# Tokens turned by products with diagonal matrices, in place of scaled tokens turned with the identity, in the opening of a hybrid encoder step

## The chip, the cores and the metric

The kernel runs on one core of one Trainium2 chip. The metric is the device time of that core in microseconds, the median of several runs. Engine names as the profile has them: PE (TensorE's matmuls), PEld (its weight loads), DVE (VectorE), ACT (ScalarE), POOL (GpSimd), SP (the engine that issues most DMAs).

## The reference

One layer of a streaming encoder, for 1024 prompt frames and 32 frames of a running stream, each of 1024 channels. What matters here is its beginning:

```python
def rmsnorm(x, g):
    xf = x.astype(jnp.float32)
    y = xf * lax.rsqrt(jnp.mean(xf * xf, axis=-1, keepdims=True) + EPS) * g.astype(jnp.float32)
    return y.astype(x.dtype)

def mixer_inputs(x, norm_g, w_in, b_f, q_g, k_g):
    h = rmsnorm(x, norm_g)
    cols = lambda a, w: h @ w_in[:, a:a + w]
    ...
    u = cols(OFF_UA, CONV_WIDTH) * jax.nn.sigmoid(cols(OFF_UB, CONV_WIDTH))
```

From h come the queries, keys and values of an attention with forget gates, the input u of a causal convolution of width 31, and gates. Attention and convolution are each gated and projected, mixed, projected once more and added to x. All of it is float32.

## The kernel before

All 1056 frames (tokens) are handled together. The kernel wants h with channels on the partitions, while x comes with tokens on the partitions. So nine tiles `xtok[t]` of 128 tokens x 1024 channels (the ninth has the 32 stream tokens) are loaded, each token is multiplied by the inverse root of its mean square, and each 128 x 128 block is turned on TensorE into PSUM. On the way out of PSUM the norm's gain is put on (`gs`, per channel) and the value is split into two float16 parts: `xh` on ScalarE (L578), and `xl`, the rest, on VectorE (L579). Every projection is then three float16 products per block of 128 channels: wh with xh, wl with xh, wh with xl (`mms`, L183), the weights being split in the same way (`high`, L138; `low`, L141).

The opening overlaps this with the first two projections (the two factors of u for its first 128 channels; weights `ws0`). `x_split(c, ...)` works on chunk c of the tokens: chunk 0 has tiles 0 and 1, chunk 1 tiles 2 to 4, chunk 2 tiles 5 to 8 (`XCH`). For each of the 8 blocks of channels (kt) it turns the chunk's tiles into one PSUM tile (`ptx`; three PSUM buffers in all), takes xh and xl out of it, runs the jobs that are listed for this kt, and then releases the products of earlier kt that have waited long enough in the lists `behind` (`drain`). In this part the order on PE, DVE and ACT is the program's order (`manual_schedule`); GpSimd and SP are ordered by the scheduler. So an instruction of PE, DVE or ACT that waits holds back all that stands behind it on that engine.

The names that the change touches:

- `squares(t)` sums a tile's squares into a column of `rs9`; `root` and `newton` make inverse roots of them in place (L530 to L532, L509 to L511). `rooted(2, 3)` does tiles 2 to 4, `rooted(5, 4)` tiles 5 to 8.
- `scale(t, h)` multiplies half h of the channels of tile t by its roots, in place, on VectorE (L541) or GpSimd (L539). There are 18: tiles 1, 3 and 6 on GpSimd, the others on VectorE.
- the turn: `nc.tensor.transpose` of a block of `xtok` with the identity `ident` (L576).

After the opening come the other projections of u, v, k, q and the gates with the convolution's taps on VectorE beside them, then the attention over heads, the layer norm, and the output projections. Two lines of them are of use for comparison: L1172, which multiplies the attention's probabilities with the values (plain float32), and

```python
    def over_channels(acc, put):
        for c in range(3):
            pm = psT.tile([128, 512], F32, name="psn", tag="T")
            nc.tensor.matmul(pm[:, :CH], ones_f, acc[:, csl(c)], start=True, stop=True)   # L1202
```

where `ones_f`, `mean` and `rstd` are float32 and CH is 352. In L1172 the inner loop runs over c in 0 to 3 and j below 2c + 2, 20 products for each of the 16 heads.

Of the kernel before, what the change touches and what calls it, by code (L numbers as in the profile page):

```python
# [8 lines left out]
F32 = mybir.dt.float32  # L9
# [5 lines left out]
ALU = mybir.AluOpType  # L15
# [38 lines left out]
def build(tc, xT, xt, wv, wf, ckT, cv, clT, stT, vec, cst, yT, kT, vO, lfO, cpT, csT):  # L54
    nc = tc.nc
# [3 lines left out]
    def pool(name, bufs=1, stack=es, **kw):  # L59
        return stack.enter_context(tc.tile_pool(name=name, bufs=bufs, reuse_waits="tile", **kw))  # L60
# [29 lines left out]
    class Batch:  # L90
# [46 lines left out]
        def high(self, i, wh, raw, ks):  # L137
            nc.scalar.mul(wh[:, ks, :], raw[:, ks, :], self.s[:, i:i + 1])  # L138

        def low(self, i, wl, wh, raw, ks):  # L140
            nc.vector.scalar_tensor_tensor(wl[:, ks, :], raw[:, ks, :], self.s[:, i:i + 1], wh[:, ks, :],  # L141
                                           op0=ALU.mult, op1=ALU.subtract)
# [35 lines left out]
    def mms(ps, w, rh, rl, sl, kts=range(KT), first=True, last=True):  # L178
        wh, wl = w[:2]
        n, N = 0, 3 * len(kts)  # L180
        for kt in kts:
            for a, b in ((wh, rh), (wl, rh), (wh, rl)):
                nc.tensor.matmul(ps, a[:, kt, :], b(kt, sl), start=(first and n == 0), stop=(last and n == N - 1))  # L183
                n += 1
# [202 lines left out]
    def pieces(o, n):  # L387

        if o + n <= T:
            return ((slice(0, n), slice(30 + o, 30 + o + n)),)  # L390
        return ((slice(0, T - o), slice(30 + o, 30 + T)), (slice(T - o, n), slice(60 + T, 60 + T + TS)))
# [40 lines left out]
    xip = pool("xip", 1, stack=xi, side="right")  # L432
    vec_t = cp.tile([128, NV], F32, name="vec_t")
    cst_t = xip.tile([128, NCST], F32, name="cst_t")
    xtok = {}
# [53 lines left out]
    ident = cp.tile([128, 128], F32, name="ident")  # L489
# [7 lines left out]
    rs9 = cp.tile([128, 9], F32, name="rs9")  # L497
# [15 lines left out]
    half = slice(0, D // 2), slice(D // 2, D)  # L513
    rows = lambda t: min(128, TT - 128 * t)
# [17 lines left out]
        nc.scalar.activation(y, y, AF.Exp, scale=-0.5)  # L532
        return lambda: newton(rs, v, y)

    def scale(t, h, pool=False):
        r = rows(t)
        x, f = xtok[t][:r, half[h]], rs9[:r, t:t + 1]
        if pool:
            nc.gpsimd.tensor_scalar(x, x, f, 1.0, op0=ALU.mult, op1=ALU.mult)  # L539
        else:  # L540
            nc.vector.tensor_scalar(x, x, f, None, op0=ALU.mult)  # L541

    behind = [], []

    def drain(lags):
        for q, n in zip(behind, lags):
            while len(q) > n:
                q.pop(0)()

    def x_split(c, ws, u, jobs):  # L550


        o, n = XCH[c]
        sl = slice(o, o + n)
        pss = [pj.tile([128, 512], F32, name="pj", tag="pj") for _ in range(2)]

        def project(i, kt):
            mms(pss[i][:, :n], ws[i], X, XL, sl, range(kt, kt + 1), kt == 0, kt == KT - 1)
            if kt < KT - 1:
                return  # L560
            if i == 0:
                for a, b in pieces(o, n):
                    nc.scalar.mul(u[:, b], pss[0][:, a], recs[0].inv)
                return
            nc.vector.tensor_scalar(ua0[:, sl], pss[1][:, :n], recs[1].inv, None, op0=ALU.mult)
            if c == 2:
                for o2, n2, a2 in PCS:
                    b = slice(30 + o2, 30 + o2 + n2)
                    nc.scalar.activation(u[:, b], u[:, b], AF.Sigmoid)
                    nc.vector.tensor_mul(u[:, b], ua0[:, a2:a2 + n2], u[:, b])  # L570

        for kt in range(KT):
            pt = tr.tile([128, 512], F32, name="ptx", tag="tr") if kt % 3 == 2 else st.tile([128, 512], F32, name="ptx", tag="st")
            for j in range((n + 127) // 128):
                r = min(128, n - 128 * j)
                nc.tensor.transpose(pt[:, 128 * j:128 * j + r],  # L576
                                    xtok[o // 128 + j][:r, 128 * kt:128 * kt + 128], ident[:r, :r])
            nc.scalar.mul(xh[:, kt, sl], pt[:, :n], gs[:, kt:kt + 1])  # L578
            nc.vector.scalar_tensor_tensor(xl[:, kt, sl], pt[:, :n], gs[:, kt:kt + 1], xh[:, kt, sl],  # L579
                                           op0=ALU.mult, op1=ALU.subtract)  # L580
            for job in jobs.get(kt, ()):
                job()
            for i in range(2):
                behind[i].append(lambda i=i, kt=kt: project(i, kt))
            drain((2, 5 if c == 0 else 2))
# [16 lines left out]
    def known(i):  # L602
        recs[i].power(psq[:, i + 1:i + 2], 1)
# [11 lines left out]
    top(0)  # L615
    total(1)
    step()
    scale(0, 0)
    scale(1, 0, True)
    scale(1, 1, True)  # L620
    scale(0, 1)
    known(0)
    steps_of = {}

    def rooted(t0, nt):
        steps_of[t0] = root(t0, nt)
# [12 lines left out]
    for f in range(8):  # L639
        if f in (2, 4, 6):  # L640
# [11 lines left out]
    b1 = plan.pop(0)  # L652
    b2 = plan[0]
    x_split(0, ws0, u0, {
        0: [lambda: high(0, 0), lambda: low(0, 0), lambda: top(1), lambda: squares(2, False)],
        1: [lambda: squares(3)],
        2: [lambda: high(0, 1), lambda: low(0, 1)],
        3: [lambda: total(2), lambda: known(1), lambda: squares(4)],
        4: [lambda: high(1, 0), lambda: low(1, 0), lambda: rooted(2, 3), lambda: high(0, 2)],
        5: [lambda: steps_of[2](), lambda: scale(2, 0), lambda: scale(3, 0, True), lambda: scale(4, 0), lambda: low(0, 2)],  # L660
        6: [lambda: scale(3, 1, True), lambda: scale(2, 1), lambda: high(1, 1), lambda: low(1, 1)],
        7: [lambda: scale(4, 1), lambda: high(1, 2), lambda: low(1, 2)]})
    x_split(1, ws0, u0, {
        0: [b1.load, b1.load, lambda: squares(5), lambda: squares(6, False)],
        1: [lambda: squares(7)],
        2: [lambda: squares(8)],
        3: [lambda: rooted(5, 4)],
        4: [lambda: steps_of[5](), lambda: scale(5, 0), lambda: scale(6, 0, True)],
        5: [lambda: scale(7, 0), lambda: scale(8, 0), lambda: scale(6, 1, True)],
        6: [lambda: scale(5, 1), lambda: scale(7, 1)],  # L670
        7: [lambda: scale(8, 1), lambda: b1.stage(0)]})
    x_split(2, ws0, u0, {0: [lambda: b1.stage(1)], 2: [consts], 3: [b1.total, b1.power],
                         4: [lambda: b1.split(0)], 5: [lambda: b1.rest(0, 0), lambda: b1.rest(0, 1)],
                         6: [lambda: b1.rest(0, 2), lambda: b1.split(1)]})
# [994 lines left out]
```

## Time and profile before

| | before |
|---|---|
| time, median of 3 runs | 1346.9 us (1346.65 to 1347.09) |
| profiled execution: its own time | 1345.89 us |
| its span, first to last instruction | 1344.1 us |
| mean granted TensorE clock | 0.996 of full speed |
| PE busy | 1312.6 us (98%) |
| DVE busy | 990.4 us (74%) |
| ACT busy | 719.0 us (53%) |
| POOL busy | 505.8 us (38%) |

The opening is the first 46 us of the span. A row of a time line gives the start in us, the duration in us, the engine, the line of the kernel, the operation, the tiles (out<-in), their shape, how many were merged into the row, and in brackets how long the engine had been idle and what ended the wait. A row of the views by line gives the count and, behind the bar, busy time in us and the mean of one in ns, then idle time in front of it with what ended it. Matmuls overlap, so their durations are longer than the distances between their starts.

### The profile page before, as it was taken

How to read it: one execution, taken by the hardware profiler on the slowest of the kernel's cores; microseconds unless marked ns; L12 is line 12 of the kernel's file. 1: busy time of each engine (PE TensorE's matmuls, PEld its weight loads, DVE VectorE, ACT ScalarE, POOL GpSimd, SP SyncE). 2: the span in 40 equal slices, each digit the busy share in tenths (PEclk: the TensorE clock that was granted, in tenths of full speed). 3: DMA queues.
4: the chain of work that ended last, by engine and by line, in shares of the span. 5: the costliest groups of instructions: out<-in, count | busy, mean ns of one | idle time of the engine just before them, and what ended most of it. 6: DMA issues, size and time to landing. Idle time of an engine off the chain costs nothing.

```text
span 1344.1 us, 24837 instructions
## 1 busy us (share of the span) xinstructions
PE 1312.6 (98%) x9383; PEld 1003.1 (75%) x9383; DVE 990.4 (74%) x1532; ACT 719.0 (53%) x1362; POOL 505.8 (38%) x548
## 2 busy tenths in 40 slices
PE   8999999999999999999889998999999999999999
PEld 5687876666666666667567766777776699999998
DVE  6797879888999997987778866655554489166664
ACT  6644555757676743455555555655555566233320
POOL 2001124547484820243433442222222158255562
PEclk8999999999999999999999999999999999999999
DMA  6343233425352463535644643565452698544462
GB/s 251 98 140 104 93 112 118 139 82 187 95 180 87 162 166 109 160 90 155 165 109 123 186 132 99 147 179 132 131 152 54 240 313 262 176 128 146 142 190 69
DMA packets 113496, 194.97 MB, mean 145 GB/s; under 512 B 34080, under 2 KB 80032, under 8 KB 113376
## 3 DMA queue, kind: packets, MB, share of 16 engines
q1 hardware_dynamic: 113232, 193.31, 46.9%
q8 instruction: 74, 1.21, 0.4%
q14 instruction: 46, 0.38, 0.1%
q10 hardware_dynamic: 144, 0.07, 0.0%
HBM read 127.68 MB, written 65.64 MB: 144 GB/s over the span
## 4 chain that ended last, share of the span: by engine, by line
PE 82%; DVE 9%; ACT 3%; issue 2%; DMA 2%; SPq 1%; POOL 0%; DVEq 0%; ACTq 0%; POOLq 0%
PE pj L183 56%; PE pjv L761 6%; PE pj L1501 6%; PE po L1172 4%; PE ptr L1153 3%; DVE nm L1126 2%; DVE wl L141 2%; DVE y L371 2%; PE psS L1122 2%; PE psS L1121 2%; DMA ga<-s_ga 2%; ACT wh L138 1%; DVE psS L1124 1%; DMA s_q<-qh 1%; PE warm L477 1%
## 5 line engine op out<-in xcount | busy, mean ns | idle before, releaser
L183 PE MATMUL pj<-xh,wh 128*128 128x352 f16 (+2 forms) x1536 | 481.6, 314 | 2.3 <-ACT wh L138 1.4
L183 PE MATMUL pj<-xh,wl 128*128 128x352 f16 (+2 forms) x1536 | 481.2, 313 | 0.7 <-DVE wl L141 0.6
L183 PE MATMUL pj<-xl,wh 128*128 128x352 f16 (+2 forms) x1536 | 480.9, 313 | 0.5 <-DVE xl L579 0.4
L183 PEld LDWEIGHTS <-wh 128*128 128x128 f16 x3072 | 301.5, 98 | 162.1 <-issue 7.1
L371 DVE SCALAR_TENSOR_TENSOR y<-u,vec_t,y 128x1086 f32<-128x1086 f32 x240 | 346.8, 1446 | 12.0 <-ACT y L368 8.9
L1139 POOL TENSOR_SCALAR P<-P,nm 128x128 f32<-128x128 f32 (+7 forms) x128 | 129.9, 1015 | 279.9 <-DVE nm L1138 229.8
L183 PEld LDWEIGHTS <-wl 128*128 128x128 f16 x1536 | 150.5, 98 | 72.0 <-DVE wl L141 1.6
L141 DVE SCALAR_TENSOR_TENSOR wl<-raw,sc,wh 128x384 f16<-128x384 f32 (+1 forms) x192 | 128.2, 693 | 48.3 <-ACT wh L138 48.3
L1133 ACT ACTIVATE P<-psS,nm 128x128 f32<-128x128 f32 (+7 forms) x128 | 95.1, 743 | 113.3 <-DVE nm L1138 70.9
L1126 DVE TENSOR_REDUCE nm<-psS 128x1 f32<-128x128 f32 (+7 forms) x128 | 97.0, 758 | 12.5
L1153 PE MATMUL ptr<-ident,P 128*128 128x128 f32 x576 | 88.6, 276 | 17.3 <-DVE pt L1156 9.2
L175 POOL TENSOR_TENSOR wl<-raw,wh 128x384 fp32r<-128x384 f32 (+1 forms) x51 | 63.3, 1270 | 74.3 <-ACT wh L172 58.6
L1153 PEld LDWEIGHTS ptr<-ident,P 128*128 128x128 f32 x576 | 69.2, 141 | 28.2 <-DVE pt L1156 12.1
L1156 ACT COPY pt<-ptr 128x512 f32<-128x512 f32 (+3 forms) x128 | 64.3, 502 | 44.4 <-PE ptr L1153 43.2
L1121 PE MATMUL psS<-KB,QB 128*128 128x256 f32 (+2 forms) x192 | 81.8, 427 | 0.6 <-ACT P L1133 0.6
L880 POOL TENSOR_TENSOR sql<-sqf,sqh 128x352 fp32r<-128x352 f32 x48 | 57.0, 1187 | 65.8 <-ACT sqh L877 65.8
L138 ACT ACTIVATE wh<-raw,sc 128x1024 f16<-128x1024 f32 (+1 forms) x68 | 73.9, 1091 | 8.2 <-DVE sc L158 7.9
L1172 PE MATMUL po<-pt,V 128*64 128x256 f32 x640 | 72.8, 382 | 2.5 <-ACT pts L1078 1.7
L1124 DVE TENSOR_TENSOR psS<-psS,cmask 128x128 f32<-128x128 f32 x128 | 37.6, 294 | 46.0 <-PE psS L1122 45.6
L906 POOL TENSOR_TENSOR ql<-qn,qh 128x352 fp32r<-128x352 f32 (+1 forms) x48 | 67.8, 1429 | 6.6 <-ACT qh L905 6.5
L761 PE MATMUL pjv<-vwh,xh 128*128 128x260 f16 x256 | 70.1, 274 | 0.0
L761 PE MATMUL pjv<-vwl,xh 128*128 128x260 f16 x256 | 70.0, 273 | 0.0
(271 smaller groups left out, 2532.9 us busy)
## 6 DMA issues: line engine op xcount, KB each, us to landing
raw<-wf SPq DMA_DIRECT2D x92, 512.0 KB
QB<-s_q SPq DMA_DIRECT2D x32, 256.0 KB
KB<-s_k SPq DMA_DIRECT2D x32, 256.0 KB
kT<-qn SPq DMA_DIRECT2D x8, 528.0 KB
s_ga<-t SPq DMA_DIRECT2D x24, 176.0 KB
s_gb<-t SPq DMA_DIRECT2D x24, 176.0 KB
s_ma<-t SPq DMA_DIRECT2D x24, 176.0 KB
s_mb<-t SPq DMA_DIRECT2D x24, 176.0 KB
```

Of the source, the lines that this page charges most:

```text
L138: nc.scalar.mul(wh[:, ks, :], raw[:, ks, :], self.s[:, i:i + 1])
L141: nc.vector.scalar_tensor_tensor(wl[:, ks, :], raw[:, ks, :], self.s[:, i:i + 1], wh[:, ks, :], op0=ALU.mult, op1=ALU.subtract)
L183: nc.tensor.matmul(ps, a[:, kt, :], b(kt, sl), start=(first and n == 0), stop=(last and n == N - 1))
L371: t = nc.vector.scalar_tensor_tensor(y, u[:, i:i + CW], w, y, op0=ALU.mult, op1=ALU.add)
L761: nc.tensor.matmul(ps[:, :VC], a, b, start=(n == 0), stop=(n == 23))
L1121: nc.tensor.matmul(ps[:, b, :wm], QB[:, qsl], KB[:, ksl], start=True, stop=False)
L1126: nc.vector.tensor_reduce(nm[:, 0:1], ps[:, :nb, :w], axis=AX.XY, op=ALU.max, negate=True)
L1133: nc.scalar.activation(P[:, :nk].rearrange("p (b w) -> p b w", b=nb), ps[:, :nb, :w], AF.Exp, bias=nm[:, 0:1], accum_out=nm[:, 1:2])
L1139: nc.gpsimd.tensor_scalar(P[:, :nk], P[:, :nk], nm[:, 2:3], 1.0, op0=ALU.mult, op1=ALU.mult)
L1153: nc.tensor.transpose(pt[:, 128 * j:128 * j + 128], P[:, 128 * (4 * u + j):128 * (4 * u + j) + 128], ident)
L1172: nc.tensor.matmul(po[rows], V[:, j, :], parts[c][:, j, :], start=(c % 2 == 0 and j < 2), stop=(c % 2 == 1 and j >= 2 * c))
L1501: nc.tensor.matmul(pss[c][:, :HC], a[:, k, :], x, start=(not more and kt == 0 and n == 0), stop=(kt == 3 and n == 2), skip_group_check=more)
```

## The change

`scale` and its 18 calls are taken out. In their place `diag(t)` writes a 128 x 128 tile with the roots of tile t on its diagonal (the identity times the root, per partition; 32 x 32 for the last tile), nine in all, on VectorE. A block of `xtok` is then turned and scaled at once, by a plain product with that diagonal tile as the moving operand instead of a turn with the identity. `xtok` itself stays as it was loaded.

```diff
-    def scale(t, h, pool=False):
-        r = rows(t)
-        x, f = xtok[t][:r, half[h]], rs9[:r, t:t + 1]
-        if pool:
-            nc.gpsimd.tensor_scalar(x, x, f, 1.0, op0=ALU.mult, op1=ALU.mult)
-        else:
-            nc.vector.tensor_scalar(x, x, f, None, op0=ALU.mult)
+    diags = {}
+
+    def diag(*ts):
+        for t in ts:
+            r = rows(t)
+            diags[t] = xip.tile([128, 128], F32, name="diag", tag="diag", bufs=9)
+            nc.vector.tensor_scalar(diags[t][:r, :r], ident[:r, :r], rs9[:r, t:t + 1], None, op0=ALU.mult)
...
             for j in range((n + 127) // 128):
                 r = min(128, n - 128 * j)
-                nc.tensor.transpose(pt[:, 128 * j:128 * j + r],
-                                    xtok[o // 128 + j][:r, 128 * kt:128 * kt + 128], ident[:r, :r])
+                t = o // 128 + j
+                nc.tensor.matmul(pt[:, 128 * j:128 * j + r], xtok[t][:r, 128 * kt:128 * kt + 128], diags[t][:r, :r],
+                                 start=True, stop=True)
...
     step()
-    scale(0, 0)
-    scale(1, 0, True)
-    scale(1, 1, True)
-    scale(0, 1)
+    diag(0, 1)
     known(0)
...
-        5: [lambda: steps_of[2](), lambda: scale(2, 0), lambda: scale(3, 0, True), lambda: scale(4, 0), lambda: low(0, 2)],
-        6: [lambda: scale(3, 1, True), lambda: scale(2, 1), lambda: high(1, 1), lambda: low(1, 1)],
-        7: [lambda: scale(4, 1), lambda: high(1, 2), lambda: low(1, 2)]})
+        5: [lambda: steps_of[2](), lambda: diag(2, 3, 4), lambda: low(0, 2)],
+        6: [lambda: high(1, 1), lambda: low(1, 1)],
+        7: [lambda: high(1, 2), lambda: low(1, 2)]})
...
-        4: [lambda: steps_of[5](), lambda: scale(5, 0), lambda: scale(6, 0, True)],
-        5: [lambda: scale(7, 0), lambda: scale(8, 0), lambda: scale(6, 1, True)],
-        6: [lambda: scale(5, 1), lambda: scale(7, 1)],
-        7: [lambda: scale(8, 1), lambda: b1.stage(0)]})
+        4: [lambda: steps_of[5](), lambda: diag(5, 6, 7, 8)],
+        7: [lambda: b1.stage(0)]})
```

## The prediction

> **What bounds the kernel now.** I read the page first, for the bound of the whole, then the chain of waits in order of time for the first 140 us, because the change lies in the first 46 us and the question is whether time lost there comes back later. The page's first part:
>
> ```profile
> PE 1312.6 (98%) x9383; PEld 1003.1 (75%) x9383; DVE 990.4 (74%) x1532; ACT 719.0 (53%) x1362; POOL 505.8 (38%) x548
> ```
>
> TensorE is busy for 98% of the span. What happens in the opening therefore moves the end only by the moment at which TensorE's unbroken work begins. The chain shows that moment (start, duration, what; the lines are those the chain went through):
>
> ```profile
> 19.26 1.33 DVE xtok L541 x2
> 20.59 0.82 DVE wl L141
> ...
> 32.49 0.78 DVE xtok L541 x2
> ...
> 46.08 17.59 PE pj L183 x114
> ```
>
> There are three stages. In chunk 0 the chain runs over VectorE and ScalarE; near its end stand two scales (L541) and a weight low part (L141), and behind them the low part xl of a turned tile (L579), which frees the PSUM buffer for the first turn of chunk 1. In chunk 1 (to 33.86, the first turn of four tiles) the chain again names scales, although TensorE is nearly full, as shown below. In chunk 2 (from 33.86) turns and products alternate on TensorE, and from 46.08 on 114 products follow without a break. So a TensorE microsecond added in chunk 2 arrives at the end whole; a VectorE microsecond removed counts only as far as it made TensorE wait.
>
> **The turn becomes a product: what one costs.** The number of instructions is the first thing to settle. The turns at L576 are 2x8 + 3x8 + 3x8 = 64 of full size (and 8 of 32 rows), and 64 MATMULs stand in the view by shape. Plain float32 products are different: the loop at L1202 has three of them for mean and the view has six MATMULs; the loop at L1172 has 16 heads x 20 = 320 and the view has 640:
>
> ```profile
> L1172 PE MATMUL po<-pt,V 128*64 128x256 f32 x640 | 72.8, 382 | 2.5 <-ACT pts L1078 1.7 <-ACT mean L1211 0.7
> ...
> L576 PE MATMUL ptx<-ident,xtok 128*128 128x128 f32 x64 | 11.9, 293 | 1.8 <-DVE xl L579 1.8
> ...
> L1202 PE MATMUL psn<-mean,ones_f 128*128 128x352 f32 x6 | 2.4, 476 | 0.0
> ```
>
> So a turn is one pass and a plain float32 product is two, each with its own weight load. xtok and the new diagonal tile are both float32, so every block becomes two passes. Now the step of a pass, from the time line of TensorE (matmuls overlap, so the step is the distance between starts, not the duration):
>
> ```profile
> 25.18 0.49 PE L576 MATMUL ptx<-ident,xtok 128*128 128x128 f32 x3
> 25.50 0.33 PE L183 MATMUL pj<-xh,wh 128*128 128x384 f16 x1
> ...
> 26.48 0.49 PE L576 MATMUL ptx<-ident,xtok 128*128 128x128 f32 x3
> ...
> 35.49 0.66 PE L576 MATMUL ptx<-ident,xtok 128*128 128x128 f32 x4
> 36.09 0.34 PE L183 MATMUL pj<-xh,wh 128*128 128x384 f16 x1
> ```
>
> Three turns take 25.50 - 25.18 = 0.32 us, 0.107 each. For a pass of a plain product, two records of L1202 cover 0.76 us and one lasts 0.459, so the second starts 0.30 after the first (the first row is from the time line, the second from the view of the line; then two rows of L1501's time line, and the loads):
>
> ```profile
> 808.97 0.76 PE L1202 MATMUL psn<-mean,ones_f 128*128 128x352 f32 x2
> L1202 PE MATMUL psn<-mean,ones_f x6: 459/459/563, 809.0 to 814.3; 128*128 128x352 f32 x6
> 1289.77 0.29 PE L1501 MATMUL pj<-ml,wh 128*128 128x264 f32 x1
> ...
> 1291.94 0.28 PE L1501 MATMUL pj<-ml,wh 128*128 128x264 f32 x1
> L1202 PEld LDWEIGHTS psn<-mean,ones_f 128*128 128x128 f32 x6 | 1.0, 189 | 0.4 <-ACT mean L1211 0.3
> ```
>
> That is 0.30 for 352 columns, so 0.109 for 128: the lower end. The upper end is the weight load, which lasts 189 ns and must overlap passes of only 128 columns. The nearest row with such loads behind short products is L1501: 18 steps from 1289.77 to 1291.94 make 0.121 each. I take 0.112, near the lower end, because the loads of L1202 overlap their passes. A block then goes from 0.107 to 0.224, **+0.117 us** (0.111 to 0.135).
>
> The Trainium skill, "Perfetto Trace Analysis", section "Optimizing Tensor Performance", asks that logical transposes use the transpose and not a standard matmul, since the transpose skips the arithmetic. It speaks against this change; the trace agrees, with one record of 0.107 against two of 0.109.
>
> **Where the added passes lie.** Chunk 0 has 16 blocks. They lie beside ScalarE's and VectorE's chain and ahead of a TensorE wait of 1.30 us (its row is below), so I put them at nothing, except those just ahead of that wait; without that cover they would cost 16 x 0.117 = 1.9. Chunk 1 has 24: its turns start at 25.18 and 26.48, a kt step of 1.30, which is three turns (0.32) and six products (0.163 each) with no hole (the first row of such a pair, 25.50, starts where the turns' steps end), so TensorE itself paces it and the added passes count. Chunk 2 has 24 full blocks and 8 of 32 rows, and is all TensorE. Full blocks on the path: 48 x 0.117 = **+5.6** (5.3 to 6.5).
>
> The 32-row block costs more than its size: four turns of chunk 2 take 36.09 - 35.49 = 0.60, so the fourth takes 0.28. Its weight load cannot slip behind the product ahead of it. A second pass needs another load with only 32 columns to hide behind; between one full pass (0.11) and the whole 0.28 less a little (0.24) I take 0.17: 8 x 0.17 = **+1.4** (0.9 to 1.9).
>
> **What the removed scales give back.** They are 12 on VectorE and 6 on GpSimd; nine diagonals replace them, on VectorE alone.
>
> ```profile
> 23.43 0.47 DVE L141 SCALAR_TENSOR_TENSOR wl<-raw,sc,wh 128x256 f16<-128x256 f32 x1
> ...
> 39.21 0.22 DVE L631 CAST bones<-cst_t 128x128 fp32r<-128x128 f32 x1
> ```
> ```profile
> 17.38 0.63 PE L576 MATMUL ptx<-ident,xtok 128*128 128x128 f32 x2
> ...
> 20.29 0.27 PE L183 MATMUL pj<-xl,wh 128*128 128x256 f16 x1
> 21.86 0.55 PE L576 MATMUL ptx<-ident,xtok 128*128 128x128 f32 x3 [1.30 <-DVE xl L579]
> ...
> 23.67 0.27 PE L183 MATMUL pj<-xh,wh 128*128 128x256 f16 x1
> 23.97 0.28 PE L183 MATMUL pj<-xh,wl 128*128 128x256 f16 x1
> ...
> 32.18 0.33 PE L183 MATMUL pj<-xh,wl 128*128 128x384 f16 x1
> 32.55 0.32 PE L183 MATMUL pj<-xl,wh 128*128 128x384 f16 x1
> ...
> 33.86 0.72 PE L576 MATMUL ptx<-ident,xtok 128*128 128x128 f32 x4 [0.50 <-DVE xl L579]
> ```
>
> A diagonal is taken at the 0.22 of a copy of the same shape (39.21). In the chain, from 19.26 on, 1.33 us of scales become three diagonals (0.66), and the weight low part behind them, 0.82 on the chain beside GpSimd's scaling, goes back to the 0.47 of its twin at 23.43. xl, next in VectorE's queue, ends 1.33 - 0.66 + 0.82 - 0.47 = 1.0 earlier, and the turn behind it could start at 20.85. TensorE's own queue ends about then: its last product ahead of the wait starts at 20.29 and takes a step of 0.11, and of the pair at 17.38, a pass of which takes 0.21 (0.63 for two records that last 0.42 each), and of the pair after it, the four added passes bring up to 0.84, or half of it where the later step of 0.11 holds already: 20.85 to 21.25. So **-1.0** (0.5 to 1.2).
>
> In chunk 1 three holes belong to work behind scales: 23.67 to 23.97 (0.19 beyond a step of 0.11), 32.18 to 32.55 (0.21 beyond 0.16), and the wait of 0.50 on xl before 33.86, ahead of which the chain shows the scales of 32.49. Four diagonals (0.9) stand where six scales at 0.39 (32.49: 0.78 for two) stood, and TensorE is slower anyway: they close, **-0.9** (0.6 to 1.1, the upper end with the 0.16 by which the products ahead of 33.86 run out).
>
> At the very start nothing is won: tile 1's turn no longer waits for GpSimd, but two passes each take that up. GpSimd loses only work that nobody else queues behind, and SP issues nothing new. The new wait is for the diagonals; behind them on VectorE are low(0,2) and xl, counted above. PSUM and the evictions (L578, L579) are as before.
>
> **The sum:** -1.0 - 0.9 + 5.6 + 1.4 = **+5.1 us**; by the ends +3.9 to +7.3. The profiled run was 1345.89 (span 1344.1), the median 1346.9, 1.0 above it. So the span should be near 1349.2, and the median 1346.9 + 5.1 = **1352.0** (1350.8 to 1354.2).
>
> **The rivals.** (1) *The product costs what the turn costs*, one pass: then only the gains stay, 1346.9 - 1.9 = 1345.0, not slower. It decides if a diagonal product shows 72 MATMULs. Against it are the doubled counts of L1172 and L1202. 6%. (2) *Chunk 1 is bound by VectorE and ScalarE*, as the chain says from 21.86 to 33.86, so its 24 blocks (2.8 us) hide: 1349.2. Against it is the step of 1.30 without holes. 7%. (3) *Four passes instead of two*: 3 x 0.107 = 0.32 more per block, 15.4 for 48, and three added passes of 0.17 on each of eight 32-row blocks, 4.1: -1.9 + 15.4 + 4.1 = +17.6, 1364.5. Nothing in the two doubled rows speaks for it. 4%. The Trainium skill, "TensorE: Matmul & The Clock Gate", section "Terms", states that transpose mode is 4x faster for float32; by that rule this rival holds, while the trace has two times. (4) *Waits later on absorb half*, because some later wait of TensorE ends by a transfer that the delay does not move: 1346.9 + 2.5 = 1349.4. The 98% and the unbroken run from 46.08 speak against it. 5%.
>
> **How the numbers follow.** The forecast has 78%. Its own ends, rival 2 and rival 4 are inside 1348.8 to 1355.2; rivals 1 and 3 and the tail of the weight loads are left out. A difference of 0.2% (2.7 us) is about what a measurement of this kernel can tell from no change. Faster by more than that: 3% (rival 1 with a larger gain). Within it, up to 1349.6: 15% (rivals 1, 2, 4 for the most part). Slower: 82%.
>
> **What would show it.** 144 MATMULs at L576, six of them about 0.67 us apart from the first to the next product in chunk 1 where three took 0.32; a kt step there of 1.65 instead of 1.30; in chunk 2 about 2.1 instead of 1.58; the first turn of chunk 1 near 21; no wait on xl before chunk 2; the run of 114 products starting near 51 instead of 46.08. I am wrong if the kt steps of chunk 1 stay at 1.30, if L576 has 72 records, or if the run starts 5 us late and the end does not.

## The result and the profile after

| | before | after |
|---|---|---|
| time, median of 17 runs each | 1350.36 us | 1352.9 us |
| ratio | | 1.0026, 95% interval 1.0015 to 1.0038 |
| span of the profiled execution | 1344.1 us | 1350.5 us |
| start of the unbroken run of products | 46.08 us | 50.51 us |

The change makes the kernel slower by 0.26%, 3.5 us (2.0 to 5.1). The median of before lies above the 1346.9 known at the time of the prediction: those three runs are the lowest of the 17 (up to 1354.46). So the ratio of the runs timed together is what counts; the two medians alone differ by 2.5 us, inside the same interval.

The page after, its first part; TensorE has 72 matmuls and 5.3 us more:

```profile
PE 1317.9 (98%) x9455; PEld 1011.3 (75%) x9455; DVE 986.8 (73%) x1529; ACT 720.2 (53%) x1362; POOL 502.1 (37%) x542
```

The chain of waits after, in order of time, at the places that were shown of before:

```profile
19.23 0.68 DVE diag L541 x3
19.91 0.40 DVE wl L141
20.30 0.41 DVE xl L580
...
20.75 0.94 PE ptx L577 x6
...
34.51 1.00 PE ptx L577 x8
...
50.51 17.59 PE pj L183 x114
...
120.19 11.19 PE pj L183 x75
```

Three diagonals (0.68) stand where 1.33 us of scales stood, the weight low part is back at 0.40, and chunk 1 begins at 20.75 instead of 21.86. From there to chunk 2 no VectorE or ScalarE work is left on the chain. The run of 114 products begins 50.51 - 46.08 = 4.43 us later. The last row has the same 75 products that started at 115.76 before, again 4.43 later, so the delay is passed on whole.

The turns after, by shape (count, busy, mean ns), and on the time line of TensorE:

```profile
L577 PE MATMUL ptx<-diag,xtok 128*128 128x128 f32 x128 | 18.0, 276 | 1.2 <-DVE xl L580 1.2
L577 PEld LDWEIGHTS ptx<-diag,xtok 128*128 128x128 f32 x128 | 16.7, 191 | 3.3 <-DVE xl L580 1.5 <-PE pj L480 0.5 <-issue 0.3
...
L577 PE MATMUL ptx<-diag,xtok 32*128 32x32 f32 x16 | 3.2, 282 | 0.0
```
```profile
32.70 0.83 PE L577 MATMUL ptx<-diag,xtok 128*128 128x128 f32 x6
33.37 0.33 PE L183 MATMUL pj<-xh,wh 128*128 128x384 f16 x1
...
34.35 1.16 PE L577 MATMUL ptx<-diag,xtok 128*128 128x128 f32 x8
35.44 0.34 PE L183 MATMUL pj<-xh,wh 128*128 128x384 f16 x1
...
36.43 1.16 PE L577 MATMUL ptx<-diag,xtok 128*128 128x128 f32 x8
```

Every block is two passes. Six passes take 33.37 - 32.70 = 0.67, 0.111 each; the step of a kt in chunk 1 is 34.35 - 32.70 = 1.65 (before 1.30), in chunk 2 36.43 - 34.35 = 2.08 (before, by the rows of the prediction, 0.60 of turns and six products, 1.58). Eight passes in chunk 2 take 1.09, so the 32-row block takes 1.09 - 0.67 = 0.42, against 0.28.

### The profile page after: what moved, and what is told of

It reads as the page before. It is cut to its first block, busy times and chain, and to the rows that moved or that the text cites. A ratio compares the mean times of both kernels' runs of the same rounds, so it can differ in the third digit from the quotient of the medians.

```text
span 1350.5 us, 24964 instructions
## 1 busy us (share of the span) xinstructions
PE 1317.9 (98%) x9455; PEld 1011.3 (75%) x9455; DVE 986.8 (73%) x1529; ACT 720.2 (53%) x1362; POOL 502.1 (37%) x542
## 3 DMA queue, kind: packets, MB, share of 16 engines
q1 hardware_dynamic: 113232, 193.31, 46.5%
## 4 chain that ended last, share of the span: by engine, by line
PE 82%; DVE 9%; ACT 3%; issue 2%; DMA 2%; POOL 0%; SPq 0%; DVEq 0%; ACTq 0%; POOLq 0%
PE pj L183 57%; PE pjv L757 6%; PE pj L1497 6%; PE po L1168 5%; PE ptr L1149 3%; DVE nm L1122 2%; DVE wl L141 2%; DVE y L371 2%; PE psS L1118 2%; PE psS L1117 2%; ACT wh L138 1%; DMA ga<-s_ga 1%; PE ptx L577 1%; DVE psS L1120 1%; DMA s_y<-y 1%
## 5 line engine op out<-in xcount | busy, mean ns | idle before, releaser
L120 POOL CAST topb<-tops 128x2 bf16<-128x2 f32 x35 | 17.9, 513 | 156.5 <-ACT junk L117 106.4
```

## The experiments

All are read at the start of the unbroken run of products after the last turn, because it repeats to 0.2 us (50.51 and 50.68 after the change, 46.08 and 46.16 before) where the whole time does not. Beside it stands the time, with its 95% interval, where a kernel was timed more than once. "The holes" are the three places in chunk 1 of the kernel before at which TensorE stands still, as the prediction lists them.

**The cost alone.** Plain products, but with the identity, and all scales left in.

```diff
-                nc.tensor.transpose(pt[:, 128 * j:128 * j + r],
-                                    xtok[o // 128 + j][:r, 128 * kt:128 * kt + 128], ident[:r, :r])
+                nc.tensor.matmul(pt[:, 128 * j:128 * j + r],
+                                 xtok[o // 128 + j][:r, 128 * kt:128 * kt + 128], ident[:r, :r],
+                                 start=True, stop=True)
```

> The cost alone: the scales stay as they were, and each block is turned by a plain product with the identity. Read at the start of the unbroken run of products after the last turn (46.08 us before, 50.51 after the change). Theory (two passes of 0.11 per block, TensorE paces chunks 1 and 2): 48 x 0.115 + 8 x 0.15 = 6.7 added, of which the holes of chunk 1 take back about 1.1, since a slower TensorE no longer meets a late VectorE: 51.7. Rival (the holes close only when the scales go): 52.8. Rival (the changed kernel's delay came from the diagonals, not from the passes): 46.1 to 47. Clock in 10 to 20 us: 1.00 if the added passes keep it up, 0.50 for 3 to 7 us if they have nothing to do with it.

The chain of waits of this kernel:

```profile
19.49 1.32 DVE xtok L541 x2
...
22.08 0.94 PE ptx L576 x6
...
51.84 17.59 PE pj L183 x114
```

51.84, which is 5.76 later than before; 51.7 was expected. The time is 1.005 of before (1.0034 to 1.0065). The scales still hold up chunk 1 (22.08), but no hole is left behind it: a slower TensorE meets a VectorE that is in time. So the delay is the passes', and the slower TensorE alone closes the holes of chunk 1. Chunk 1 itself begins 0.22 later than before (22.08 against 21.86).

**The same number of passes, as turns.** Each block is turned twice.

```diff
+                for _ in range(2):
                     nc.tensor.transpose(...)
```

> Each block is turned twice with the identity into the same place, scales as before: as many passes on TensorE as the products have, but all in transpose mode. Theory (a pass is a pass): the run of products starts within 0.3 us of the kernel with products with the identity, near 51.5. On the clock: if only the share of busy time counts, 1.00 from 10 to 20 us as in the changed kernel; if turns do not count as work (the Trainium skill, TensorE: Matmul & The Clock Gate, Part 4), 0.50 in part of it, as before.

The run of products starts at 50.69, 4.61 later than before and 1.15 earlier than with products; "within 0.3 us" was wrong. Most of the difference stands in chunk 2, in the eight passes of one kt:

```profile
35.40 1.05 PE L577 MATMUL ptx<-ident,xtok 128*128 128x128 f32 x8
L577 PEld LDWEIGHTS ptx<-ident,xtok 128*128 128x128 f32 x128 | 15.0, 141 | 4.8 <-DVE xl L580 2.6 <-PE pj L480 0.5 <-issue 0.3
```

1.05 is 0.11 less than the 1.16 of a product's eight, 0.9 over the eight kt. A turn's weight load lasts 141 ns, a product's 191, and for the 32-row block 135 and 182. That the difference of the loads shows in that block, where the second load has only 32 columns to hide behind, is read from these rows and was not tested by a run of its own. The rest stands ahead of chunk 2: one or two hundredths a kt in the full blocks, and 0.1 in the start of chunk 1 (22.08 against 21.96). So of a product's extra over one turn, four fifths (4.61 of 5.76) is the second pass as such, and one fifth goes, by this reading, to the longer weight load, above all in the short block. This kernel was run once.

**The gain alone.** The changed kernel with turns in place of the products; no token is scaled then.

```diff
-                nc.tensor.matmul(pt[...], xtok[t][:r, 128 * kt:128 * kt + 128], diags[t][:r, :r],
-                                 start=True, stop=True)
+                nc.tensor.transpose(pt[...], xtok[t][:r, 128 * kt:128 * kt + 128], ident[:r, :r])
```

> The gain alone: the changed kernel with turns by the identity in place of the products; the diagonals are still made, but no token is scaled, so that part of the computation is left out. Theory: chunk 1 starts at 20.75 as in the changed kernel and has no holes, so the run of products starts at 46.08 - 1.1 - 1.1 = 43.9 (43.6 to 44.3), and the time is about 2.2 us (0.16%) below before. Rival (the holes of chunk 1 close only because TensorE is slower in the changed kernel): 45.0. Clock in 10 to 20 us: below 1.00 in some part if the turns leave it too little work.

```profile
20.49 0.55 PE ptx L577 x3
...
29.81 0.82 DVE diag L541 x4
30.62 0.53 DVE xl L579
...
44.02 17.59 PE pj L183 x114
```

44.02: 2.06 earlier than before, 43.9 expected. Chunk 1 starts 1.37 earlier; the holes give only 0.7, since xl is still on the chain at 30.62, now behind the four diagonals. The rest of the holes, about 0.5, closes in the changed kernel because TensorE is slower there, so the rival is half right. The time is 0.9992 of before (0.9977 to 1.0007), which can't be told from no change. With the run before: cost 5.76 and gain 2.06 make 3.70, and the change makes 4.43, because the 0.7 of the holes is counted in both.

**Chunk 0 alone.** Diagonal products for tiles 0 and 1, scales and turns for the others.

```diff
+                if t < 2:
+                    nc.tensor.matmul(pt[...], xtok[t][:r, 128 * kt:128 * kt + 128],
+                                     diags[t][:r, :r], start=True, stop=True)
+                    continue
                 nc.tensor.transpose(...)
...
-    scale(0, 0)
-    scale(1, 0, True)
-    scale(1, 1, True)
-    scale(0, 1)
+    diag(0, 1)
```

> Diagonal products for tiles 0 and 1 only (chunk 0), scales and turns for the rest. Theory (chunk 0's 16 added passes lie under ScalarE's and VectorE's chain): the run of products starts at 46.0 to 46.2, as before. Rival (they push chunk 1 by their length): 46.08 + 1.8 = 47.9. Clock in 10 to 20 us: 1.00 if the added passes of chunk 0 keep it up.

Chunk 1 starts at 21.83 (before 21.86): the 16 added passes of chunk 0 are hidden, as expected. But the run of products starts at 47.32, 1.24 later, between theory and rival. The view by stretches (from and to, length, then busy time and count of PE, PEld, DVE, ACT and POOL, the granted clock, the DMA share and GB/s) shows why:

```profile
19.34:22.75 3.41, 1.13 (x9) 0.67 (x7) 3.41 (x7) 0.84 (x3) 1.76 (x2) 1.00 1.04 415
22.75:26.16 3.41, 3.41 (x18) 2.60 (x18) 2.80 (x6) 1.48 (x4) 0.00 (x0) 0.50 0.23 93
```

TensorE had waited most of 3.4 us, 2.28 of them ahead of chunk 1 (before 1.30), and for the next 3.4 it got half its clock, in chunk 1 where it sets the pace. The half clock of before (13.14 to 19.97) lay in chunk 0. One profile does not show that the stretch moved because of the change in chunk 0; the last section compares the others.

**The 32-row block.** The kernel before, with the ninth tile filled up with zeros and turned in full.

```diff
         xtok[t] = xip.tile([128, D], F32, name="xtok", tag="xtok", bufs=9)
+        if r < 128:
+            nc.gpsimd.memset(xtok[t], 0.0)
...
-                nc.tensor.transpose(pt[:, 128 * j:128 * j + r],
-                                    xtok[o // 128 + j][:r, 128 * kt:128 * kt + 128], ident[:r, :r])
+                nc.tensor.transpose(pt[:, 128 * j:128 * j + 128],
+                                    xtok[o // 128 + j][:, 128 * kt:128 * kt + 128], ident)
```

> The kernel before, with the ninth token tile filled up to 128 rows with zeros, so that its eight blocks are turned in full instead of with 32 rows. Theory (the 32-row block costs 0.28 us because its weight load cannot start beside the work of other rows): a full turn takes 0.109, so 8 x 0.17 = 1.4 us less in chunk 2, and the run of products starts at 44.7 instead of 46.08. Rival (the block's cost is its size plus a fixed latency): 46.1 to 46.5. If a half clock falls into chunk 1, up to 1.7 more.

```profile
35.28 0.60 PE L578 MATMUL ptx<-ident,xtok 128*128 128x128 f32 x4
35.71 0.33 PE L183 MATMUL pj<-xh,wh 128*128 128x384 f16 x1
```

Four full turns take 35.71 - 35.28 = 0.43, against 0.60 with the short one, and the run of products starts at 44.84 by its chain, 1.24 earlier than before; the 75 products that stand at 115.76 in before stand at 114.42, 1.34 earlier, as forecast. A block with four times the rows is the cheaper one; the rival, 46.1 to 46.5, is out. Why the short one is dear the run does not show. Time: 0.9989 (0.9977 to 1.0001).

**A version from these,** against the changed kernel. Diagonal products only for tiles 0 and 1 and for the first two kt of chunk 1; the other channels of tiles 2 to 4 scaled in chunk 1, tiles 5 to 8 one kt earlier than before, the ninth tile padded.

```diff
+                if t < 2 or (t < 5 and kt < 2):
+                    nc.tensor.matmul(pt[...], xtok[t][...], diags[t][:r, :r], start=True, stop=True)
+                    continue
+                nc.tensor.transpose(pt[:, 128 * j:128 * j + 128], xtok[t][:, 128 * kt:128 * kt + 128], ident)
...
-        0: [b1.load, b1.load, lambda: squares(5), lambda: squares(6, False)],
-        1: [lambda: squares(7)],
+        0: [b1.load, b1.load, lambda: squares(5), lambda: scale(2, 2), lambda: scale(3, 2), lambda: scale(4, 2),
+            lambda: squares(6, False)],
+        1: [lambda: squares(7), lambda: scale(2, 1), lambda: scale(3, 1), lambda: scale(4, 1)],
...
-        3: [lambda: rooted(5, 4)],
+        3: [lambda: rooted(5, 4), lambda: steps_of[5](), lambda: scale(6, 0, True), lambda: scale(5, 0)],
...
```

Here `scale(t, 2)` is the second quarter of the channels.

> Diagonal products only where TensorE waits or where the scales come too late: chunk 0, and the first two kt of chunk 1. The other channels of tiles 2 to 4 are scaled in place a little later, tiles 5 to 8 as before but one kt earlier, and the ninth tile is padded. Theory: chunk 1 starts at 20.75 as in the changed kernel; 2 x 3 x 0.115 = 0.7 is paid; the holes of chunk 1 (1.2) mostly close; chunk 2 gets 1.4 shorter: 46.08 - 1.1 + 0.7 - 1.0 - 1.4 = 43.3 (43.0 to 44.0), about 2.8 us or 0.2% under before. Rival (the removed scales never were on the path): 46.08 + 0.7 - 1.4 = 45.4. With a half clock in chunk 1, up to 1.7 more.

> The kernel with few diagonal products once more, because its ratio of 0.9964 is more than the 1.5 us (0.11%) that its opening shows. Theory (the time beyond the opening varies from run to run and does not belong to the change): a ratio nearer 0.9985, with the run of products at 44.56 again. Rival (the shorter opening wins more later on): again 0.9964, and a profile whose stretches after 570 us are shorter than before's.

The run of products starts at 44.56 and 44.50, and the 75 products of 115.76 at 114.14 and 114.08, 1.6 and 1.7 us earlier than in before: 2.8 was expected. The second profile's chain has scales still there at the end of chunk 1:

```profile
30.79 0.78 DVE xtok L543 x2
...
32.10 0.79 DVE xtok L543 x2
...
44.50 17.48 PE pj L183 x114
```

The times are 0.9964 (0.9951 to 0.9977) and, once more with more runs, 0.9979 (0.9968 to 0.9990), so it is faster than both kernels. The opening accounts for 1.7 us, 0.13%, which is inside the second interval and short of the first; what the rest is, if it is more than spread, these runs don't show. Of the 1.7, padding the ninth tile alone brought 1.24 (44.84): the few products and the earlier scales add 0.3. Chunk 1 begins 1.1 earlier (20.79 and 20.73), its products cost 0.7 by the forecast, and ahead of chunk 2 TensorE still waits 0.51 us for an xl behind the scales, as before.

**The scales of the second halves moved on into chunk 2.**

```diff
-        4: [lambda: scale(7, 0), lambda: scale(8, 0), lambda: scale(6, 1, True)],
-        5: [lambda: scale(5, 1), lambda: scale(7, 1)],
-        6: [lambda: scale(8, 1)],
+        4: [lambda: scale(7, 0), lambda: scale(8, 0, True)],
...
-    x_split(2, ws0, u0, {0: [lambda: b1.stage(1)], 2: [consts],
+    x_split(2, ws0, u0, {0: [lambda: b1.stage(1), lambda: scale(6, 1, True), lambda: scale(5, 1)],
+                         1: [lambda: scale(7, 1), lambda: scale(8, 1)], 2: [consts],
```

> The kernel with few diagonal products, with the scales of the second half of the channels of tiles 5 to 8 moved into chunk 2, and one more scale on GpSimd. Theory (the 1.2 us of holes that were left ahead of chunk 2 come from six scales in VectorE's queue at the end of chunk 1; two remain): the run of products starts at 43.6 to 44.0 instead of 44.56. Rival (GpSimd's scaling beside VectorE slows it as much as is saved): 44.5. The time: 0.15 to 0.3% below before by the opening.

```profile
32.11 0.58 ACT xh L592
32.69 1.04 ACT junk L117 x2
33.73 0.50 ACT xh L592
34.23 1.04 ACT junk L117 x2
...
36.45 0.78 DVE xtok L543 x2
...
37.75 0.57 DVE xl L593
...
44.53 17.48 PE pj L183 x114
```

44.53, nothing won; 43.6 to 44.0 was expected. The scales did leave the place ahead of chunk 2: its first turns start at 32.89 instead of 33.53, without a wait. But two of the moved scales (36.45) now stand on the chain inside chunk 2, ahead of an xl for which TensorE waits 0.56 us (to 38.37), a wait that the version before it has not. ScalarE's two sums of squares of the next weights (L117, 1.04 each), which stand between two xh, are on the chain ahead of them. So the wait moved by one stage. The rival named the right time, but nothing shows its reason: the two scales at 36.45 take 0.39 each, as they did before, and GpSimd is idle then. Time: 0.999 (0.9977 to 1.0002).

**Both kernels once more,** for what comes after the opening.

> The changed kernel once more. Theory (the opening's delay is in the program, what follows differs from run to run): the run of products starts at 50.5 again, or up to 1.7 later where a half clock falls into chunk 1; the delay stays the same to the microsecond's hundredth up to about 570 us, and the 2.0 us that came on top near 821 us in the first profile come out differently. Rival (the 2.0 us are the change's too): the same delay of 6.4 at the end.

> The kernel before once more. Theory: the run of products starts at 46.1, or up to 1.7 later where a half clock falls into chunk 1; the stretches after 570 us differ from its first profile by some tenths to 2 us without any change in the program. Rival (one profile repeats the other): 46.08 and 1344.1.

The run of products starts at 50.68 and 46.16. The time of the changed kernel is again 1.0029 of before (1.0014 to 1.0043). In the repeat of the changed kernel the delay stays at 4.59 up to 570 us. Behind that, the view by line gives the first and the last start of one kind of products (before, then before once more):

```profile
L1049 PE MATMUL psS<-kc,qs_t x32: 589/601/613, 652.0 to 1010.6; 64*32 64x512 f32 x32
```
```profile
L1049 PE MATMUL psS<-kc,qs_t x32: 588/613/1060, 653.0 to 1013.3; 64*32 64x512 f32 x32
```

The last one starts at 1010.6 in one profile and at 1013.3 in the other, with the same program and openings 0.08 apart. So the 2.0 us that the first profile after had on top of 4.43 (span 1350.5 against 1344.1) are within what two executions of one kernel differ by in the attention, and nothing shows that they belong to the change. The granted clock can account for most of them: near 830 us it is 0.50 from 825.5 to 828.9 in the first profile of before, and from 836.8 to 843.6 in the first after. That is 3.41 us more at half clock, which costs up to 1.7. The repeat of before has a half clock from 647.8 to 654.6 that its first profile has not. The rival, the same 6.4 again, is out: the repeat ends 7.6 behind the first profile of before, and 5.0 behind the second. Behind the opening, those two repeats have their half clock at the same places of the program (from 647.8 and 835.5 us, and from 653.8 and 841.6), and their runs of products start 4.52 apart.

## Why the prediction was right

**Two passes per block** was right: 128 and 16 records. **The step of a pass** was put at 0.112 and is 0.111; the added cost of a full block 0.115 against 0.117, so 48 blocks cost 5.5 against 5.6. That the longer weight load would hide in a full block was right as well. **The 32-row block** was put at +0.17 and is +0.14 to 0.15 (0.42 against 0.28): 1.2 us against 1.4.

**Where the passes lie:** chunk 0 hides its own (chunk 1 at 21.83 with diagonals in chunk 0 alone; 0.1 to 0.2 later with two passes and all scales), and chunks 1 and 2 pay in full, by their steps of 1.65 and 2.08 against the forecast 1.65 and 2.1. Rival 2, by which chunk 1 belongs to VectorE as the chain said, is out: the chain names the work behind which TensorE last waited, and the step without holes told better.

**The gain ahead of chunk 1** was put at 1.0 and is 1.11: three diagonals took 0.68 for the 0.66 assumed, and the weight low part fell by 0.42 where 0.35 was counted. The late end of TensorE's own queue, which bounded it, did not come: the queue ended at 19.4, since the clock was at full in this profile. **The holes** gave about 1.1 to 1.2 against 0.9. The prediction named both causes, the missing scales and the slower TensorE; the scales' going alone gave 0.7, the slower TensorE alone all of it. The sum is 5.5 + 1.2 - 1.1 - 1.2 = 4.4 against +5.1: all four terms erred a little, all to the slow side. The measured 3.5 (2.0 to 5.1) holds the 4.43 of the opening, and the forecast at its upper edge. That the median came out at 1352.9, so near the 1352.0 that was forecast, is partly luck: the 1346.9 from which it was counted was 3.5 too low, and the difference of the medians was 2.5 where 5.1 was forecast.

**Rivals 1 and 3** (one pass, four passes) fall with the counts and the 0.111: 4x, as the Trainium skill, "TensorE: Matmul & The Clock Gate", section "Terms", has it for the transpose mode in float32, is two times here (0.222 against 0.107). **Rival 4**, absorption by later waits, is out up to 570 us, where the delay is the same to 0.02 us. Behind that the executions differ by more than it could have taken away, but of the two repeats, alike in their half clock behind the opening, the changed one ends 5.0 later: half of the delay was not absorbed there.

## What to carry to other kernels

Before work is moved from VectorE or GpSimd onto TensorE, count the records of a like operation in the trace per call: a plain float32 product is two passes with two weight loads where a turn is one. Price the moved work stage by stage by TensorE's step, and not by the chain alone: where the step has no holes, added passes count in full even if the chain names another engine. And look for the short block first: padding it was worth 1.24 us here, while starting the late scales earlier and replacing only the first blocks' turns added 0.3, and moving scales on moved the wait with them.

## What was not expected of the hardware

**Half clock after an idle stretch, and turns count as work.** The granted clock went to 0.50 for 3.41 or 6.83 us behind stretches of 3.41 us in which TensorE had little to do. Within a profile its changes lie whole multiples of 3.41 us apart (before, from 13.14 to 825.51 are 238 of 3.4133), so a stretch can be placed also where the clock did not change. Here is the same place of the program in two kernels, each with the stretch that followed: products with the identity, where the clock fell, and turns done twice, where it did not (placed from its half clock at 836.86, 241 stretches on):

```profile
14.19:17.60 3.41, 1.87 (x13) 1.14 (x13) 2.47 (x8) 2.62 (x8) 0.26 (x1) 1.00 1.08 316
17.60:21.02 3.42, 3.42 (x19) 2.80 (x18) 2.42 (x7) 2.26 (x7) 1.41 (x2) 0.50 1.01 402
```
```profile
14.25:17.66 3.41, 1.98 (x15) 1.24 (x15) 2.31 (x7) 2.62 (x8) 0.27 (x1) 1.00 1.06 339
17.66:21.08 3.42, 2.01 (x19) 1.60 (x17) 2.60 (x7) 2.31 (x6) 1.59 (x2) 1.00 1.03 410
```

13 passes were too few here and 15 enough. Of the 15 in the second kernel, 8 are turns (four from 14.29 on, four from 17.32 on); if they did not count, 7 would have been left, fewer than the 13 that were too few. But the count is no threshold: before, a stretch with 15 records, two of them products of one column, was followed by half clock, and in the version with few diagonal products one of 13 (14.00 to 17.41) was not. The Trainium skill, "TensorE: Matmul & The Clock Gate", Part 4, states that the transpose mode does not count as busy in the same way; these stretches, one profile of each kernel, speak against it. The stretch before:

```profile
9.73:13.14 3.41, 1.99 (x15) 1.31 (x14) 2.75 (x6) 3.41 (x8) 0.66 (x2) 1.00 1.03 412
13.14:16.55 3.41, 2.60 (x12) 1.35 (x10) 2.44 (x7) 3.14 (x8) 0.27 (x1) 0.50 1.02 381
```

Over all profiles, the clock fell within chunk 0 in each of the four with one turn per block there (before twice, no token scaled, padded), and in one of the eight with two passes per block, that of the products with the identity. So the added passes of chunk 0, which delayed chunk 1 by 0.2 us at most, mostly kept the clock up there. When the stretches begin differs from execution to execution (before, the half clock began at 13.14 and at 12.91), so half a clock can fall into chunk 0, where VectorE and ScalarE are on the chain (before: 13.14 to 19.97), or into chunk 1, where it cost 1.24 us (diagonals in chunk 0 alone).

**A short block is dearer than a full one.** The turn of 32 rows took 0.28 us behind full ones, a turn of 128 rows 0.11. In the kernel before, the weight loads (PEld) stand idle for 0.17 us ahead of the short block's load and wait for nothing that the profile shows; the row of the full blocks' loads has no such wait. Why, the runs don't show.

```profile
35.34 0.41 PEld L576 LDWEIGHTS ptx<-ident,xtok 128*128 128x128 f32 x3
35.91 0.13 PEld L576 LDWEIGHTS ptx<-ident,xtok 32*128 32x128 f32 x1 [0.17 <-issue]
```
